# Buffers of their own for some streamed weights, and work laid into other places, in a hybrid SSD and attention decoder block

## The chip, the cores and the metric

The kernel runs on one core of a Trainium2 chip. The metric is the device time of one execution in microseconds (us). A core has five engines that this text names: PE (TensorE, the matrix products), DVE (VectorE), ACT (ScalarE), POOL (GpSimd) and SP (SyncE, which here does nothing but issue DMA transfers). Each engine works through its own instructions in order and waits at a semaphore where it needs another's result. "Issued in order" holds for SP as well: a transfer that must wait for its buffer holds up all that stand behind it in SP's queue.

## The reference, cut to what matters

One decoder block, sequence 1024, width 1024, everything in float32:

```
h     = rms_norm(x) * (1 + sc1) + sh1                  # sc, sh, g from the condition c
z, xbc, dt, q, k, v, gates = split(h @ w_in)
y_ssd = ssd_branch(z, xbc, dt)                         # causal conv, softplus(dt), chunked scan, silu(z), norm
y_att = diff_attention_branch(q, k, v)                 # rope, causal softmax, difference of two heads, norm
merged = sig(gate_ssd) * (y_ssd @ w_ssd_o) + sig(gate_att) * (y_att @ w_attn_o)
x  = x + g1 * rms_norm(merged @ w_out)
h2 = rms_norm(x) * (1 + sc2) + sh2
u  = causal_dwconv(h2 @ w_up)                          # 3 taps, 2 * 2816 channels
x  = x + g2 * rms_norm((gelu(u_gate) * u_val) @ w_down)
```

Inside the SSD branch, `dt = softplus(dt_raw + dt_bias)`, `la = -dt * exp(a_log)` and its running sum `acum` over chunks of 128 give the decays.

## The kernel before, in words

**Products.** A float32 product is made of three products in the rounded type fp32r: `split(hi, lo, raw)` (lines 93 and 94) lets ACT copy `raw` to a rounded `hi` and DVE subtract to get `lo`; `mm3` (lines 115 to 117) issues hi·hi, hi·lo and lo·hi into the same PSUM bank. Weights come by SP's DMA queue as a raw piece of 128 partitions x 1024, and are split. Most pieces rotate through pools: three buffers with the tag `wraw`, four each for `whi` and `wlo`. A load into a `wraw` buffer waits until the split has read what was there.

**Slots.** Longer-lived tensors take one of 43 slots (128 x 1024 float32) from `SL`: `get` takes the front of a list of free slots, `put` appends to its end. A tensor that takes a slot waits for whoever used it last, and which slot it is depends on all gets and puts before it.

**Order.** Inside `manual_schedule(engines=...)` the instructions of the named engines stay in the order in which the code is written; elsewhere a scheduler lays them out. Of the stages below, z is manual on PE, DVE, ACT and SP. The stages in order of time in the trace: h and first products (0 to 75 us), xbc and others (75 to 214), z (214 to 331), the SSD scan and v (from 331), gates, q and k, attention, attention's output product (about 1100 to 1185), the product with `w_out` ("mix"), norm and h2, the up-projection (about 1290 to 1712), the down-projection (to the end).

**z** (lines 529 to 578) runs over three thirds of the columns (346, 346, 348); each third needs four pieces of weights (`kp` 0 to 3, each two blocks of 128 rows), and runs over eight token tiles `i` of 24 matmuls. `fetch_z` loads a piece (line 531), `split_z` splits it. Three pieces of the next third are fetched at tile 1, and split after tile 7; the fourth is fetched after the first split, which frees its buffer. After each tile ACT takes a tanh (line 574), DVE a product (575), in the first third also the dt columns (570), and SP stores the result (576). In the second third three functions are called after tiles 1, 3 and 5: `decays_a` (23 elementwise operations, lines 484 to 503), `decays_b` (two matmuls that sum `la` along the chunk, 505 to 517), `decays_c` (eight transposes, 519 to 525). POOL sums parts of w_down (lines 415 to 418) beside all this.

**Start of the scan.** After z the slots of `ev`, `wdr` and `wds` go back to the list, and `yt`, `xd`, `xdd`, `xtk`, `M`, ... take slots.

**Attention's output product** "ao" (lines 1300 to 1321) runs over eight blocks `j` of two halves with 24 matmuls each. `fetch_ao` (1189) loads the weights `wao` two blocks ahead, `split_ao` splits them. `gth` (1303) and `mst` (1304) are loaded per block; DVE merges (1319, 1320) into `mt`, which is split into `mT[j][half]`, the operand of mix. Beside it, in blocks 0 to 2 `early_load` brings two pieces of w_up (`ws`, 1283) and `early_sums` makes four sums of them on DVE (1288 to 1291), stored to memory; in blocks 3 to 6 a piece of `w_out` (`wo`, 1313) is loaded and split. All of these use the three `wraw` buffers.

**Up-projection**: 22 pairs `m` of blocks, each made in seven products `p` (a Strassen-like scheme) of 12 matmuls into banks X, Z, X, Y, X, Y, X; ACT and DVE combine the banks (lines 1826 to 1849: `cv`, `evs`, `cg`). A pair's conv steps (`up_conv` 0 to 4: steps 0 and 2 start with an ACT pass, line 1436, all of 0 to 3 have a DVE tap, 1437, then gelu, 1439; step 4 multiplies, 1441, and stores, 1446 and 1447) and its four sums (`up_gsum`, 1455, stored 1457) are laid into places (m, p) of later pairs. For the early pairs that is the list `early` (lines 1804 to 1811). The last pair's are in the list `rest` (1868), inside the first of the down products.

**Down-projection**: seven products over six pieces `kp`; 24 matmuls per full piece. `left_part` (line 1756) loads a piece of the gelu product or its sums back through two `gst` buffers and splits it; `right_part` loads from w_down (`wdb`) or from POOL's sums (`wdt`, 1767).

Of the kernel before, what the change touches and what calls it, by code (L numbers as in the profile page):

```python
# [17 lines left out]
P = 128  # L18
# [43 lines left out]
def kernel(ctx: ExitStack, tc: tile.TileContext, a: dict, out: bass.AP, dbg=None):  # L62
# [422 lines left out]
    def decays_a():  # L485
        t0 = f(sp0_)
        t1 = sp1_
        x_ = f(dtr)
        V.scalar_tensor_tensor(t0, x_, -1.0, x_, op0=ALU.mult, op1=ALU.min)
        A.activation(t0, t0, AF.Exp)  # L490
        V.tensor_scalar(t1, t0, 2.0, None, op0=ALU.add)
        V.reciprocal(t1, t1)
        V.tensor_tensor(t0, t0, t1, op=ALU.mult)
        V.tensor_tensor(t1, t0, t0, op=ALU.mult)
        dtf = f(dt)
        V.tensor_scalar(dtf, t1, 2.0 / 15, 2.0 / 13, op0=ALU.mult, op1=ALU.add)
        for m in (11, 9, 7, 5, 3, 1):
            V.tensor_tensor(dtf, dtf, t1, op=ALU.mult)
            V.tensor_scalar(dtf, dtf, 2.0 / m, None, op0=ALU.add)
        V.tensor_tensor(dtf, dtf, t0, op=ALU.mult)  # L500
        V.scalar_tensor_tensor(dtf, x_, 0.0, dtf, op0=ALU.max, op1=ALU.add)
        A.activation(aexp, rows[:, R_AL : R_AL + NH], AF.Exp)
        V.scalar_tensor_tensor(la, dt, -1.0, aexp[:, None, :].broadcast_to([P, 8, NH]), op0=ALU.mult, op1=ALU.mult)

# [21 lines left out]

    thirds = ((0, 346), (346, 346), (692, 348))
# [12 lines left out]
    z_raw = [fetch_z(*thirds[0], kp) for kp in range(3)]  # L540
    with tc.manual_schedule(engines={EN.PE, EN.DVE, EN.Activation, EN.SP}):
        for t_, (c0, wdt) in enumerate(thirds):
            if t_ == 0:
                wz = []
                for kp in range(4):
                    wz.append(split_z(c0, wdt, kp, z_raw.pop(0)))
                    if kp == 0:
                        z_raw.append(fetch_z(c0, wdt, 3))
            else:
                wz = wz_next  # L550
            for i in range(8):
# [7 lines left out]
                if t_ < 2 and i == 1:  # L559
                    z_raw = [fetch_z(*thirds[t_ + 1], kp) for kp in range(3)]  # L560
                if t_ < 2 and i == 7:
                    wz_next = []
                    for kp in range(4):
                        wz_next.append(split_z(*thirds[t_ + 1], kp, z_raw.pop(0)))
                        if kp == 0:
                            z_raw.append(fetch_z(*thirds[t_ + 1], 3))
# [634 lines left out]
    with tc.manual_schedule(engines={EN.PE, EN.DVE, EN.Activation, EN.Pool}):  # L1201
# [71 lines left out]
        mT = [[new_hl(f"mT{k}_{h}") for h in range(2)] for k in range(KD)]  # L1273
# [728 lines left out]
```

## Time and profile before

| | |
|---|---|
| median of 3 runs | 1930.75 us (1929.4 to 1933.46) |
| profiled execution | 1933.49 us, span in the trace 1931.7 us |
| TensorE's mean granted clock | 0.99 |
| PE busy | 1869.5 us, 97% of the span |
| DVE, ACT, POOL busy | 1209.6, 850.4, 215.4 us |
| DMA | 309.48 MB, mean 160 GB/s |

Times in the profile are microseconds from the start of the span. "L531" is line 531 of the program; "out<-in" names the tensors. "idle before <-releaser" tells how long an engine had waited and whose work ended the wait. PE stands for the matmuls, PEld for the weight loads that run beside them; PEclk is the clock that the throttle granted to TensorE, 1.00 being full speed. SPq is the time in which SP issues a transfer; a DMA row in the chain of waits is the time from issue to landing.

### The profile page before, as it was taken

What the parts mean: (1) busy time and instruction counts of PE and PEld (TensorE: products, weight loads), DVE (VectorE), ACT (ScalarE), POOL (GpSimd) and SP (SyncE); (2) the same over time, 40 slices, a digit from 0 to 9 for tenths busy, and PEclk for the clock granted to TensorE, in tenths of its full rate; (3) what the DMA queues carried; (4) which work ended last, traced back from release to release, by engine and by line L of the source; (5) the groups of instructions that cost most, each with busy time, mean ns of one, the idle gap of its engine ahead of it and who ended that gap; (6) DMA issues with size and microseconds to landing.
All of it is one profiled execution on the core that took longest, in us unless ns stands there. A gap on an engine that the chain in (4) does not pass through costs nothing.

```text
span 1931.7 us, 24508 instructions
## 1 busy us (share of the span) xinstructions
PE 1869.5 (97%) x9128; PEld 1560.1 (81%) x9128; DVE 1209.6 (63%) x1815; ACT 850.4 (44%) x1628; POOL 215.4 (11%) x225
## 2 busy tenths in 40 slices
PE   6999979999999999999999999999999999999998
PEld 4787978788888888888888778887788888878886
DVE  6957343575326326667767546368998888886545
ACT  5522122655313215565556413266555455455532
POOL 0000252454261000000000010100000000000001
PEclk8999989999999999999999999999999999999999
DMA  9834365142666745665572368122332232368754
GB/s 304 275 112 144 120 207 174 51 136 80 248 234 147 242 168 152 176 178 154 158 191 81 111 229 284 69 84 77 115 109 103 104 115 92 108 228 290 244 156 158
DMA packets 135575, 309.48 MB, mean 160 GB/s; under 512 B 17056, under 2 KB 48416, under 8 KB 135456
## 3 DMA queue, kind: packets, MB, share of 16 engines
q1 hardware_dynamic: 127808, 281.65, 45.5%
q0 software_dynamic: 7648, 26.26, 3.9%
q8 instruction: 72, 1.18, 0.2%
q14 instruction: 47, 0.39, 0.1%
HBM read 218.97 MB, written 88.88 MB: 159 GB/s over the span
## 4 chain that ended last, share of the span: by engine, by line
PE 80%; DVE 8%; ACT 5%; DMA 4%; issue 2%; SPq 1%; POOL 0%; POOLq 0%; ACTq 0%; DVEq 0%
PE upx L1420 4%; PE upx L1421 4%; PE upx L1419 3%; PE o L1125 3%; PE xbc L115 2%; PE xbc L116 2%; PE xbc L117 2%; PE upy L1420 2%; PE upy L1419 2%; PE upy L1421 2%; PE dx L1783 2%; PE dx L1784 2%; PE dx L1782 2%; PE dy L1784 2%; PE dy L1782 2%
## 5 line engine op out<-in xcount | busy, mean ns | idle before, releaser
L1419 PE MATMUL upx<-t,wu_t 128*128 128x512 f32 x264 | 103.2, 391 | 1.5 <-DVE cv L1845 1.5
L1420 PE MATMUL upx<-t,wu_t 128*128 128x512 f32 x264 | 102.8, 390 | 0.2 <-DVE t L1537 0.2
L1421 PE MATMUL upx<-t,wu_t 128*128 128x512 f32 x264 | 102.8, 389 | 0.0
L1113 ACT COPY aT<-at 128x512 f32<-128x512 f32 (+2 forms) x96 | 46.1, 481 | 103.1 <-PE at L1112 103.1
L1393 ACT ACTIVATE wu_t<-sab 128x512 fp32r<-128x512 f32 x57 | 34.1, 628 | 124.6 <-DVE sab L1410 124.6
L1125 PEld LDWEIGHTS o<-vt,aT 128*128 128x128 f32 x576 | 74.6, 191 | 10.1 <-ACT aT L1113 6.1
L1125 PE MATMUL o<-vt,aT 128*128 128x128 f32 x576 | 80.9, 277 | 0.5 <-ACT aT L1113 0.3
L94 DVE TENSOR_TENSOR g_lo<-gst,g_hi 128x1024 fp32r<-128x1024 f32 (+1 forms) x42 | 47.6, 1134 | 45.0 <-ACT g_hi L93 44.9
L142 POOL TENSOR_TENSOR rsf<-rsf,nhalf 128x1 f32<-128x1 f32 x8 | 5.6, 705 | 627.3 <-DVE rsf L141 624.6
L115 PE MATMUL z<-wz_hi,hT 128*128 128x346 f32 (+1 forms) x192 | 65.2, 339 | 7.5 <-ACT wz_hi L93 7.5
L93 ACT ACTIVATE g_hi<-gst 128x1024 fp32r<-128x1024 f32 (+1 forms) x42 | 41.6, 990 | 64.9 <-DMA gst<-gld_s 28.3
L142 POOL TENSOR_TENSOR sqt<-sqt,nhalf 128x4 f32<-128x4 f32 x16 | 16.6, 1035 | 465.6 <-DVE sqt L141 465.6
L1086 DVE TENSOR_REDUCE nmx<-sc 128x1 f32<-128x640 f32 (+3 forms) x64 | 65.6, 1025 | 2.2
L116 PE MATMUL z<-wz_lo,hT 128*128 128x346 f32 (+1 forms) x192 | 64.7, 337 | 1.7 <-DVE wz_lo L94 1.7
L117 PE MATMUL z<-wz_hi,hT 128*128 128x346 f32 (+1 forms) x192 | 64.1, 334 | 0.0
L1066 PE MATMUL sc<-kst,qst 128*128 128x512 f32 (+2 forms) x192 | 63.8, 340 | 0.0
L115 PE MATMUL xbc<-hT,wx_hi 128*128 128x512 f32 x160 | 63.5, 397 | 0.0
L1067 PE MATMUL sc<-klo,qst 128*128 128x512 f32 (+2 forms) x192 | 63.2, 346 | 0.0
L117 PE MATMUL xbc<-hT,wx_lo 128*128 128x512 f32 x160 | 62.3, 389 | 0.0
L116 PE MATMUL xbc<-hT,wx_hi 128*128 128x512 f32 x160 | 62.2, 389 | 0.0
L1437 DVE SCALAR_TENSOR_TENSOR ug<-cg,vec,ug 128x1023 f32<-128x1023 f32 (+1 forms) x44 | 56.3, 1281 | 6.1 <-ACT ug L1436 5.0
L1419 PEld LDWEIGHTS upx<-t,wu_t 128*128 128x128 f32 x264 | 49.6, 188 | 12.9 <-DVE cv L1845 2.6
(449 smaller groups left out, 5859.0 us busy)
## 6 DMA issues: line engine op xcount, KB each, us to landing
adas<-in_w_ada SPq DMA_DIRECT2D x32, 512.0 KB, 5.0
wdr<-in_w_down POOLq DMA_DIRECT2D x22, 512.0 KB, 7.0
wtd<-wds POOLq DMA_DIRECT2D x22, 512.0 KB, 4.6
wuf<-in_w_up SPq DMA_DIRECT2D x22, 512.0 KB, 3.5
gld_s<-gsum SPq DMA_DIRECT2D x22, 512.0 KB, 2.8
gst<-gld_s SPq DMA_DIRECT2D x20, 512.0 KB, 4.4
wdt_raw<-wtd SPq DMA_DIRECT2D x20, 512.0 KB, 4.7
wuv<-in_w_up SPq DMA_DIRECT2D x19, 512.0 KB, 3.6
```

The source lines that it names most:

```text
L115: T.matmul(ps, lh, rh, start=(i == 0), stop=False)
L116: T.matmul(ps, lh, rl, start=False, stop=False)
L117: T.matmul(ps, ll, rh, start=False, stop=(i == n - 1))
L1066: T.matmul(sc[:, n0:n1], qs_[s][:, tsl], ks_[s][:, n0:n1], start=True, stop=False)
L1067: T.matmul(sc[:, n0:n1], qs_[s][:, tsl], kl[s][:, n0:n1], start=False, stop=True)
L1086: V.reduce_max(nmx[:, bq, s : s + 1], sc[:, :L], axis=AX.X, negate=True)
L1125: T.matmul(po_of[j, grp][:, qi, :], at[:, k, :], vt[j % 2][:, kt, :], start=(kt == 0), stop=(kt == i))
L1419: T.matmul(out_, wh, xh_, start=(k == 0 and first), stop=False, skip_group_check=not first)
L1420: T.matmul(out_, wh, xl_, start=False, stop=False, skip_group_check=not first)
L1421: T.matmul(out_, wl, xh_, start=False, stop=(k == end), skip_group_check=not first)
L1782: T.matmul(o, gh[:, kk, tsl], wh, start=(k == 0 and not more), stop=False, skip_group_check=more)
L1784: T.matmul(o, gl[:, kk, tsl], wh, start=False, stop=(k == KF - 1), skip_group_check=more)
```

## The change

It has five parts, called A to E in what follows.

A. z's fourth piece gets a slot of its own, `zraw`, taken before the block and put back after it, and is fetched together with the other three.

```diff
     def fetch_z(c0, wdt, kp):
-        raw = wp.tile([P, 2, wdt], F32, tag="wraw", name=f"wz{c0}_{kp}_raw", bufs=3)
+        raw = zraw[:, :, :wdt] if kp == 3 else wp.tile([P, 2, wdt], F32, tag="wraw", name=f"wz{c0}_{kp}_raw", bufs=3)
...
-    z_raw = [fetch_z(*thirds[0], kp) for kp in range(3)]
+    zraw = SL.get("zraw", F32, (P, 2, HALF))
+    z_raw = [fetch_z(*thirds[0], kp) for kp in range(4)]
...
                 if t_ < 2 and i == 1:
-                    z_raw = [fetch_z(*thirds[t_ + 1], kp) for kp in range(3)]
+                    z_raw = [fetch_z(*thirds[t_ + 1], kp) for kp in range(4)]
                 if t_ < 2 and i == 7:
                     wz_next = []
                     for kp in range(4):
                         wz_next.append(split_z(*thirds[t_ + 1], kp, z_raw.pop(0)))
-                        if kp == 0:
-                            z_raw.append(fetch_z(*thirds[t_ + 1], 3))
...
-    SL.put(*ev, *wdr, *wds)
+    SL.put(*ev, *wdr, *wds, zraw)
```

B. `decays_a` becomes a generator with a `yield` after each of its operations; six of them are issued after each of the tiles 0 to 4 of the second third. `decays_b` follows tile 6, `decays_c` tile 1 of the last third.

```diff
-                if t_ == 1 and i in (1, 3, 5):
-                    (decays_a, decays_b, decays_c)[i // 2]()
+                if t_ == 1 and i < 5:
+                    dec = dec or decays_a()
+                    for _ in range(6):
+                        next(dec, None)
+                elif t_ == 1 and i == 6:
+                    assert next(dec, None) is None
+                    decays_b()
+                elif t_ == 2 and i == 1:
+                    decays_c()
```

SP's queue in the first third of z: the stores `zd` of its tiles and the four loads for the second third (the last third's stand alike). Before:

```order
L576 DMA zd_622<-ev_1614 128x330
L531 DMA wz_0_raw<-in_w_zdt 128x2x346
L531 DMA wz_1_raw<-in_w_zdt 128x2x346
L531 DMA wz_2_raw<-in_w_zdt 128x2x346
L576 DMA zd_623<-ev_1615 128x330
L576 DMA zd_624<-ev_1614 128x330
L576 DMA zd_625<-ev_1615 128x330
L576 DMA zd_626<-ev_1614 128x330
L576 DMA zd_627<-ev_1615 128x330
L576 DMA zd_628<-ev_1614 128x330
L531 DMA wz_3_raw<-in_w_zdt 128x2x346
L576 DMA zd_629<-ev_1615 128x330
```

After:

```order
L587 DMA zd_622<-ev_1614 128x330
L545 DMA wz_0_raw<-in_w_zdt 128x2x346
L545 DMA wz_1_raw<-in_w_zdt 128x2x346
L545 DMA wz_2_raw<-in_w_zdt 128x2x346
L545 DMA zraw<-in_w_zdt 128x2x346
L587 DMA zd_623<-ev_1615 128x330
L587 DMA zd_624<-ev_1614 128x330
```

The fourth load moved up by six stores, to stand with the other three.

C. In ao, the `ws` loads and the second half's `wo` pieces get slots of their own, a pair of `ws` is summed one block after its load, `wo` is loaded two pieces ahead, and `mT`'s slots are taken block by block.

```diff
-        mT = [[new_hl(f"mT{k}_{h}") for h in range(2)] for k in range(KD)]
+        mT = [[None] * 2 for _ in range(KD)]
...
-            ra, rb = [wp.tile([P, 2, HALF], F32, tag="wraw", name=f"ws{m}_{i}", bufs=3) for i in range(2)]
+            ra, rb = [SL.get(f"ws{m}_{i}", F32, (P, 2, HALF)) for i in range(2)]
...
+        def wo_load(kp):
+            if kp < 4:
+                wo_raw.append(SL.get(f"wo1_{kp}_raw", F32, (P, 2, HALF)))
+                SP.dma_start(wo_raw[-1], a["w_out"][2 * kp * P : (2 * kp + 2) * P, HALF:].rearrange("(k p) c -> p k c", p=P))
...
             if j < 3:
-                early_sums(j, *early_load(j))
-            elif j < 7:
-                kp = j - 3
-                raw = wp.tile([P, 2, HALF], F32, tag="wraw", name=f"wo1_{kp}_raw", bufs=3)
-                SP.dma_start(raw, a["w_out"][2 * kp * P : (2 * kp + 2) * P, HALF:].rearrange("(k p) c -> p k c", p=P))
+                ws_raw.append(early_load(j))
+            if 0 < j < 4:
+                early_sums(j - 1, *ws_raw.popleft())
+            if j == 3:
+                wo_load(0)
+                wo_load(1)
+            elif j > 3:
+                kp = j - 4
                 wo[1][kp] = (new_hl(f"wo1_{kp}_hi"), new_hl(f"wo1_{kp}_lo"))
+                raw = wo_raw.popleft()
                 split(*wo[1][kp], raw)
+                SL.put(raw)
+                wo_load(kp + 2)
```

SP's queue around the start of ao. `stg` loads attention's outputs back, `gad` holds the gates. Before:

```order
L1171 DMA stg_8245<-atd_676 128x512
L1028 DMA gad_660<-gev 128x512
L1304 DMA mst<-msd_662 128x1024
L1028 DMA gad_661<-gev 128x512
L1303 DMA gth_8784<-gad_654 128x1024
L1283 DMA ws_0_8822<-in_w_up 128x1024
L1028 DMA gad_661<-gev 128x512
L1283 DMA ws_1_8823<-in_w_up 128x1024
L1189 DMA wao_raw<-in_w_attn_o 128x1024
L1283 DMA ws_0_8899<-in_w_up 128x1024
L1303 DMA gth_8784<-gad_655 128x1024
L1304 DMA mst<-msd_663 128x1024
```

After:

```order
L1189 DMA stg_8243<-atd_676 128x512
L1046 DMA gad_660<-gev 128x512
L1301 DMA ws_0_8954<-in_w_up 128x1024
L1324 DMA wo_0_raw<-in_w_out 128x2x512
L1324 DMA wo_2_raw<-in_w_out 128x2x512
L1301 DMA ws_0_8875<-in_w_up 128x1024
L1046 DMA gad_661<-gev 128x512
L1301 DMA ws_1_8955<-in_w_up 128x1024
L1207 DMA wao_raw<-in_w_attn_o 128x1024
L1324 DMA wo_1_raw<-in_w_out 128x2x512
L1046 DMA gad_661<-gev 128x512
L1324 DMA wo_3_raw<-in_w_out 128x2x512
```

All six `ws` and the four `wo` loads now stand ahead of the second block's `gth` load; before, three of the six `ws` stood ahead of it, the others among the loads of blocks 1 and 2, and the `wo` at blocks 3 to 6.

D. The list for early pairs has 26 entries instead of 25.

```diff
-        early = [[x_] for x_ in early] + [[(up_conv, 1, 4), (up_gsum, 1, 0)], [(up_gsum, 1, i) for i in range(1, 4)]]
-        early += [[(up_conv, 2, i)] for i in range(5)] + [[(up_conv, 3, i)] for i in range(4)]
-        early += [[(up_conv, 3, 4), (up_gsum, 3, 0)], [(up_gsum, 3, 1), (up_gsum, 3, 2)], [(up_conv, 4, 0), (up_gsum, 3, 3)]]
-        early += [[(up_conv, 4, i)] for i in range(1, 5)]
+        early = [[x_] for x_ in early] + [[(up_conv, 1, 4)], [(up_gsum, 1, 0), (up_gsum, 1, 1)], [(up_gsum, 1, 2), (up_gsum, 1, 3)]]
+        early += [[(up_conv, 2, i)] for i in range(5)] + [[(up_conv, 3, i)] for i in range(5)]
+        early += [[(up_gsum, 3, 0), (up_gsum, 3, 1)], [(up_gsum, 3, 2), (up_conv, 4, 0)], [(up_conv, 4, 1), (up_gsum, 3, 3)]]
+        early += [[(up_conv, 4, i)] for i in range(2, 4)] + [[(up_conv, 4, 4), (up_conv, 5, 0)]]
```

From pair 3 on a step comes one or two products later. In pair 5, for instance, the first steps of conv 4 stood at products 2 and 3 and stand at 3 and 4. ACT's order there, `ug` being the pass of the conv step, the rows on line 1842 (1875) the copy of bank Y. Before:

```order
L1826 COPY cv_10261<-upx_10687 128x512
L1828 COPY evs_10039<-upx_10823 128x512
L1393 ACTIVATE wu_t_10860<-sab_10443 128x512
L1393 ACTIVATE wu_b_10881<-sab_10443 128x512
L1436 ACTIVATE ug_10444<-cg_10260,vec 128x1024
L1839 COPY evs_10039<-upx_10823 128x512
L1393 ACTIVATE wu_t_10902<-wuv_10726 128x512
L1842 COPY evs_10039<-upy_10888 128x512
```

After:

```order
L1859 COPY cv_10259<-upx_10684 128x512
L1861 COPY evs_10037<-upx_10820 128x512
L1426 ACTIVATE wu_t_10854<-sab_10441 128x512
L1426 ACTIVATE wu_b_10875<-sab_10441 128x512
L1872 COPY evs_10037<-upx_10820 128x512
L1426 ACTIVATE wu_t_10895<-wuv_10721 128x512
L1469 ACTIVATE ug_10442<-cg_10258,vec 128x1024
L1875 COPY evs_10037<-upy_10881 128x512
```

The pass `ug` moved from ahead of the copy of X to right ahead of the copy of Y.

E. The last pair's steps are spread over six pieces of the first down product instead of four.

```diff
-        rest = [[(up_conv, m, 0), (up_conv, m, 1)], [(up_conv, m, 2), (up_conv, m, 3)], [(up_conv, m, 4), (up_gsum, m, 0), (up_gsum, m, 1)], [(up_gsum, m, 2), (up_gsum, m, 3)]]
+        rest = [[(up_conv, m, i)] for i in range(4)] + [[(up_conv, m, 4), (up_gsum, m, 0)], [(up_gsum, m, i) for i in range(1, 4)]]
```

More of the change, by code (lines that the diff above doesn't have):

```diff
@@ L546 @@
                     wz.append(split_z(c0, wdt, kp, z_raw.pop(0)))
-                    if kp == 0:
-                        z_raw.append(fetch_z(c0, wdt, 3))
             else:
@@ L564 @@
                         wz_next.append(split_z(*thirds[t_ + 1], kp, z_raw.pop(0)))
-                        if kp == 0:
-                            z_raw.append(fetch_z(*thirds[t_ + 1], 3))
                 lo = 0
@@ L1294, in early_sums @@
                 G.dma_start(wsd[m][i][:, 1], y_)
+            SL.put(ra, rb)
         gth = SL.get("gth2")
@@ L1299 @@
         fetch_ao(1)
+        ws_raw, wo_raw = deque(), deque()
+        def wo_load(kp):
+            if kp < 4:
+                wo_raw.append(SL.get(f"wo1_{kp}_raw", F32, (P, 2, HALF)))
+                SP.dma_start(wo_raw[-1], a["w_out"][2 * kp * P : (2 * kp + 2) * P, HALF:].rearrange("(k p) c -> p k c", p=P))
         for j in range(KD):
@@ L1320 @@
                 V.tensor_tensor(mt[:, hsl], mt[:, hsl], mst[:, hsl], op=ALU.add)
+                mT[j][half] = new_hl(f"mT{j}_{half}")
                 split(mT[j][half][:, 0, :], mT[j][half][:, 1, :], mt[:, hsl])
@@ L1878 @@
                         left_part(1, kp)
-                    for f_, *x_ in rest[kp] if kp < len(rest) else ():
+                    for f_, *x_ in rest[kp]:
                         f_(*x_)
```

16 lines of the change are left out of this document (15 added, 1 removed).

## The prediction

> **What bounds the kernel now.** I read the busy shares first, then the waits of TensorE (PE), then the chain of waits and timelines at the places the change touches. The page:
>
> ```profile
> span 1931.7 us, 24508 instructions
> PE 1869.5 (97%) x9128; PEld 1560.1 (81%) x9128; DVE 1209.6 (63%) x1815; ACT 850.4 (44%) x1628; POOL 215.4 (11%) x225
> PE 80%; DVE 8%; ACT 5%; DMA 4%; issue 2%; SPq 1%; POOL 0%; POOLq 0%; ACTq 0%; DVEq 0%
> ```
>
> PE is the bound: 97% busy. The change leaves every matmul in, so time can only come out of PE's idle stretches and out of matmuls that ran slowly behind them. PE's waits (us in total, times, longest):
>
> ```profile
> PE z L115 <- ACT wz_hi L93: 7.5, 2, 4.7
> PE acum_ps L507 <- DVE sm L503: 5.3, 1, 5.3
> PE ao L115 <- ACT wao_hi L93: 4.5, 2, 4.2
> PE pb L711 <- ACT M L715: 1.7, 1, 1.7
> PE upx L1419 <- DVE cv L1845: 1.5, 2, 1.3
> PE dx L1783 <- DVE wdb_lo L94: 1.3, 1, 1.3
> ```
>
> The first three belong to the stages that parts A, B and C edit. What a wait costs on top is seen in the stretches around them (us, then PE, PEld, DVE, ACT, POOL busy, PE's granted clock, DMA share, GB/s):
>
> ```profile
> 251.20:258.00 6.80, 4.57 (x14) 4.20 (x15) 2.37 (x4) 1.69 (x3) 6.16 (x8) 0.50 0.15 56
> 271.60:278.50 6.90, 4.92 (x18) 4.92 (x19) 3.75 (x11) 0.79 (x3) 2.91 (x5) 0.51 0.73 232
> 299.00:305.80 6.80, 6.06 (x21) 6.06 (x22) 1.63 (x3) 0.46 (x1) 2.88 (x3) 0.50 0.71 250
> 1144.00:1152.50 8.50, 3.83 (x10) 2.63 (x10) 3.90 (x5) 2.19 (x3) 0.54 (x1) 0.80 0.86 293
> ```
>
> After each long wait the clock is half for about 6.8 us, which loses up to 3.4 us of full speed; in the fourth row 0.80 over 8.5 us is one half-clock stretch of 3.4 us, a loss of 1.7. That is why the waits alone (some 15 us in z) understate z.
>
> **Part A and B, z.** The chain of waits (start, us, what):
>
> ```profile
> 243.25 0.89 DVE wz_lo L94
> 244.16 7.71 DMA wz_raw<-in_w_zdt
> 251.95 0.79 ACT wz_hi L93
> 252.76 1.28 DVE wz_lo L94
> ...
> 267.12 1.21 DVE sm L499
> ...
> 273.24 0.30 DVE sm L503
> 273.58 0.79 PE acum_ps L507 x2
> ...
> 291.55 5.78 DMA wz_raw<-in_w_zdt
> ...
> 298.23 1.47 DVE wz_lo L94
> ```
>
> The fourth transfer of a third is issued at 244.16, only when the split of the first piece has ended and freed a buffer; it takes 7.71 us, and PE meets the split at 251.95. At 291.55 the same again. At 273.24 PE waits for decays_a's last piece, since acum's matmuls stand in PE's order two tiles behind a chain of 23 operations, two of them on ACT, the rest on DVE. What all of it costs is read from ACT's tanh rows, which mark the tiles:
>
> ```profile
> 237.95 0.45 ACT L574 ACTIVATE ev<-z 128x330 f32<-128x330 f32 x1 [3.35 <-DVE sm L570]
> 241.75 0.45 ACT L574 ACTIVATE ev<-z 128x330 f32<-128x330 f32 x1 [3.35 <-DVE sm L570]
> 326.30 0.46 ACT L574 ACTIVATE ev<-z 128x348 f32<-128x348 f32 x1 [3.32 <-PE z L117]
> ```
>
> An undisturbed tile takes 241.75 − 237.95 = 3.80 us. From tile 6 of the first third (241.75) to tile 6 of the last (326.30) are 16 tiles: 84.55 us instead of 60.8, so 23.75 lost. About 1.6 of it are the matmuls of acum and acT at full clock (rows 0.79 and 0.43, the first at half clock, and as many again for acT), which stay. Left to win: 22 (the first third's fourth piece is asked for before the block and costs PE nothing today).
>
> Does it go? With its own slot the fourth piece is issued at tile 1, six tiles or some 23 us before its split; 7.71 us fit. The split must still wait for the last product of tile 7 to free the split buffer (four of them); then ACT 0.79 and DVE 0.89 to 1.47 follow, and PE needs it after six of the next tile's eight row blocks, 3.80 × 6/8 = 2.85 us later. So 0.6 to 1.2 us are spare: no stall, but a thin margin. The decays: six operations per tile of 3.80 us, mostly 0.3 us, at worst 1.21 (row 267.12), so 1.8 to 7.3 us in a tile where DVE otherwise works some 0.7. At the worst price they run past a tile, but the two PSUM buffers and two tiles up to decays_b (tile 6) absorb it. Behind those pieces wait the tanh products and the release of PSUM; a tile's own DVE work comes first in the order. I take A and B at −22, bounds −23.75 (all loss goes) and −14 (one wait of 4.7 with its 3.4 of clock stays, 8.1 less).
>
> A's price: one slot more is taken and put back, so later tensors get another slot.
>
> ```profile
> 330.86 0.59 ACT L696 COPY xtk<-px 128x512 f32<-128x512 f32 x1
> ...
> 336.82 1.14 ACT L715 ACTIVATE M<-pb,sm 128x128 f32<-128x128 f32 x4 [2.76 <-DMA zd<-ev]
> ```
>
> M takes today the slot of the last z tile and waits for its store to land, while the xtk copy at 330.86 went ahead. One slot on, it is xtk that waits for the store: its 0.59 and a copy of 0.27 behind it come after the landing, +0.9 (0 to +2.7, the wait shown, if more falls behind it). It ends in PE's pb wait of 1.7.
>
> By the Trainium skill, GPSIMD Engine Reference, "1. Specifications", GpSimd shares its SBUF interface with VectorE and contends with instructions that have two SBUF inputs; that speaks against A, whose last lo split has two. The trace agrees: 0.89 at 243.25, and 1.28 at 252.76, in the stretch from 251 with POOL busy 6.16 of 6.80 us. By the rule alone, with POOL's work on that split, the margin is the 0.6 and not the 1.2; a kept wait would make it 1914, which is the second rival below.
>
> **Part C, the output product.** VectorE's rows at block 0 and block 5, and the chain's transfer:
>
> ```profile
> 1111.54 0.69 DVE L1319 SCALAR_TENSOR_TENSOR mt<-gth,ao 128x512 f32<-128x512 f32 x1 [1.67 <-PE ao L117]
> 1175.26 0.69 DVE L1319 SCALAR_TENSOR_TENSOR mt<-gth,ao 128x512 f32<-128x512 f32 x1 [0.83 <-PE ao L117]
> ...
> 1133.16 6.48 DMA ws<-in_w_up
> ```
>
> A 512-column matmul has a pitch of 0.2267 (twelve in 2.72 us, from 1402.19 to 1404.91 below). Five blocks of 48 are 54.4 us; 63.72 passed, 9.3 lost, of which seven mix matmuls laid between take 1.6. The ws loads wait for wraw buffers and land 6.48 us later, VectorE stands in front of its sum, and everything behind it on DVE, SP and ACT (mt, gth, the wao load, the wao split) is late: PE waits 4.5 and then runs at 0.80. Now the ws and wo loads have slots and go out in SP's order ahead of this stage, and a sum comes one block after its load. All of the wao path then keeps its usual lead. −7.2 (0.5 of small waits kept), bounds −9.3 and 0.
>
> What SP is moved past: ten loads of 512 KB now stand earlier among stg, gad and wao loads. At the 293 GB/s of the row at 1144 they are 5.2 MB, 18 us of transfer; they cost nothing as long as the loads behind them are due later than that. mT's slots are now taken block by block, which frees slots and delays nothing.
>
> **Part D, early pairs.** No work is added; conv steps and sums move one to three products later, so pair 3's cv copy no longer stands behind three sums (wait 1.3 goes, 0.2 stays). Pair 5:
>
> ```profile
> 1397.41 1.25 ACT L1436 ACTIVATE ug<-cg,vec 128x1024 f32<-128x1024 f32 x1 [1.44 <-DVE gsum L1455]
> 1398.57 0.56 ACT L1839 COPY evs<-upx 128x512 f32<-128x512 f32 x1
> 1399.71 0.59 ACT L1842 COPY evs<-upy 128x512 f32<-128x512 f32 x1
> ...
> 1402.19 0.39 PE L1419 MATMUL upy<-b,wu_b 128*128 128x512 f32 x1
> 1404.91 0.42 PE L1419 MATMUL upx<-t,wu_t 128*128 128x512 f32 x1
> ```
>
> Today ug's ACT pass goes ahead of both copies of banks, and the Y copy ends at 1400.30, 1.9 before PE needs Y at 1402.19. Now ug stands directly before the Y copy and itself waits for a sum (two DVE sums of 0.7, then 1.25 and 0.59): done about 1402.8, PE waits 0.6. The cv copy of the next product and pair 6 lose about 1 each, pairs 3 and 4 some 0.4 each. Sum +3.6 − 1.3 = +2.3; bounds −1.3 (none is late) and +4 (each copy late by one ACT pass, 1.25 × 4, less 1.3).
>
> **Part E, the last pair.** Two kp steps later (2 × 24 × 0.2267 = 10.9 us) a12's last column is stored.
>
> ```profile
> 1725.37 4.57 DMA gst<-gld_a
> 1731.06 1.23 DVE g_lo L94
> ...
> 1761.31 0.43 SPq L1767 DMA_DIRECT2D wdt_raw<-wtd  x1
> ...
> 1769.50 1.06 ACT L93 ACTIVATE wdt_hi<-wdt_raw 128x1024 fp32r<-128x1024 f32 x1 [3.35 <-DMA wdt_raw<-wtd]
> 1774.05 0.39 PE L1782 MATMUL dx<-wdt_hi,g_hi 128*128 128x512 f32 x1
> ```
>
> The wait of 1.3 in the first product (behind the product and sums of the pair) goes. But the left operands run through two gst buffers, a round of 4.57 + 1.06 + 1.23 = 6.9, 3.4 for each piece. SP's queue now holds one such piece more ahead of the first wdt load (1761.31 today). wdt_hi is ready at 1770.56, 3.5 before 1774.05, lo about 2.2 before. One piece and the 0.5 of issue: 3.9 later than today, so PE waits 1.7 for lo; with the later g_hi behind it 3.3. Net +2 with the 1.3 taken off; bounds −1.3 (no new wait) and +3.4 (two pieces: 6.9 − 2.2 = 4.7, less 1.3).
>
> **Sum.** −22 − 7.2 + 0.9 + 2.3 + 2 = −24.0. The profiled execution took 1933.49 (span 1931.7 and 1.8 around it), 2.7 above the median of 1930.75; its own time becomes 1909.5, the median 1906.8: 1907.
>
> **Rivals.**
> - Nothing is given back: the slots move nobody, copies and wdt arrive in time. −22 − 7.2 − 1.3 − 1.3 = −31.8: 1899. For it: the new waits are small against spare times of 1.9 and 2.2; against it: three queues (ACT, DVE, SP) each would have to hide it.
> - One of the large waits stays: the lo split of the fourth piece misses its 0.6 us, or the wao loads stay late in a stretch at 0.86 of DMA capacity. One wait of 4.2 to 4.7 with its slow clock, 6 to 8: 1914. Against it: 23 us of lead.
> - A new wait lets the clock fall too. The smallest wait here that was followed by half clock is z's second, 7.5 − 4.7 = 2.8 us (stretch from 299); a wdt wait of 3.3 would do it and cost 3.4 more: 1912. By the Trainium skill, TensorE: Matmul & The Clock Gate, "What's actually happening", an idle window of about 3.4 us, free-running, throttles, and as long a busy one releases; by that a wait of 2 us alone would not. The rows (0.50 after 4.7 and 2.8) neither need nor refuse the windows being fixed in time.
> - Slower: the ten moved loads stand in SP's queue waiting for slots that attention still uses, and wao, gth and stg loads behind them come late, with PE waiting. C's 7.2 is then not won, and A, B, D, E leave −16.8; it decides when the block keeps PE over 16.8 us. All 18 us of transfer with 3.4 of half clock behind them give +4.6: 1935. For it: the order has all ten ahead of the second block's gth load. Against it: DMA moved 56 to 293 GB/s in the stretches shown, so there is room, and a transfer of 6 to 8 us has a lead of tens.
> - The change moves nothing: the scheduler gives the loads their old places, and another buffer than wraw binds the fourth split: 1931. The order shows the loads moved, so only z could stand still.
>
> **How the numbers follow.** The forecast case has 0.70 (1902 to 1910 by itself, from D's and E's bounds); nothing given back 0.09; one wait stays 0.08; the clock falls as well 0.08; no change 0.03; slower 0.02. 0.2% is 3.9 us, about what a measurement of this kernel can tell from no change; all but the last two cases lie over it: faster 0.95, same 0.03, slower 0.02. The range reaches from the case without givebacks, 1899, to 1917: one kept wait at its dearest (8.1) and 2 of D's upper bound above the forecast.
>
> **What would show it.** Right: no PE wait on wz_hi or acum_ps in z, tiles of 3.80 us throughout and a clock of 1.00 from 225 to 310; ao without the wait on wao_hi; small waits on evs or cv in pairs 3 to 6 and on wdt_hi or wdt_lo at the third down product. Wrong: waits of over 2 us in z or ao again, a wait of ao on gth or wao with SP held at a ws load, or a new wait of over 4 us in the tail.

## The result, and the profile after

The changed kernel took 1905.93 us (median of four runs, 1905.24 to 1907.22), the kernel before 1930.52 on the same chip (four runs, 1929.4 to 1933.46). The ratio is 0.9871 with a 95% interval of 0.9854 to 0.9888, so 24.6 us or 1.3% faster. The forecast was 1907.

The page of the changed kernel, with the clock that the throttle granted in 40 slices (every slice at 9 now; before, two of the first seven stood at 8):

```profile
span 1903.5 us, 24513 instructions
PE 1860.1 (98%) x9128; PEld 1552.4 (82%) x9128; DVE 1205.6 (63%) x1815; ACT 848.8 (45%) x1628; POOL 213.0 (11%) x225
PEclk9999999999999999999999999999999999999999
```

PE's waits after (us in total, times, longest), those in the stages that the change touches:

```profile
PE px L711 <- DVE sm L716: 1.9, 1, 1.9
PE upy L1452 <- ACT evs L1875: 1.3, 2, 1.1
PE upx L1452 <- DVE cv L1878: 1.0, 2, 0.8
PE upx L1452 <- ACT evs L1872: 0.6, 1, 0.6
PE dx L1816 <- DVE wdb_lo L94: 0.4, 1, 0.4
```

The three large ones (wz_hi 7.5, acum_ps 5.3, wao_hi 4.5) are gone. Four of the five small ones stand where the prediction put a loss; the wait for wdb_lo, which it said would go, is left with 0.4. Two of z's stretches that ran at half clock, now (columns as before: us; PE, PEld, DVE, ACT, POOL busy; PE's clock; DMA share; GB/s):

```profile
251.20:258.00 6.80, 6.80 (x45) 6.80 (x44) 5.97 (x10) 1.47 (x4) 5.79 (x7) 1.00 0.90 269
299.00:305.80 6.80, 6.80 (x45) 6.80 (x45) 1.14 (x3) 1.70 (x4) 0.10 (x1) 1.00 0.45 180
```

PE is busy for all of both at full clock, with 45 matmuls where 14 and 21 stood.

By stages (from the first matmul of one stage to the first of the next, z to the start of its last, in the two profiled executions; worked out from the starts of PE's rows):

| stage | before | after | difference |
|---|---|---|---|
| up to z | 214.29 | 214.82 | +0.5 |
| z, first to last matmul | 115.44 | 92.69 | −22.7 |
| start of the scan, to its first product | 12.37 | 12.79 | +0.4 |
| scan to the end of attention | 758.36 | 758.15 | −0.2 |
| ao and mix | 151.90 | 144.16 | −7.7 |
| norm and h2 | 34.26 | 34.26 | 0.0 |
| up-projection | 425.73 | 428.40 | +2.7 |
| down-projection to the end | 219.38 | 218.18 | −1.2 |
| span | 1931.7 | 1903.5 | −28.2 |

The spans differ by 28.2, the medians by 24.6. The profiled execution of before was the slowest of its four (1933.46 as timed, 2.9 above their median), that of after the fastest (0.7 below): 3.6 of the difference lie in which executions were profiled. In which stage before lost its 2.9 is not known, as only one of its executions has a trace.

### The profile page after: what moved, and what is told of

Read it like the earlier page. It is cut to its first block, busy times and chain, and to the rows that moved or that the text cites. A ratio compares the mean times of both kernels' runs of the same rounds, so it can differ in the third digit from the quotient of the medians.

```text
span 1903.5 us, 24513 instructions
## 1 busy us (share of the span) xinstructions
PE 1860.1 (98%) x9128; PEld 1552.4 (82%) x9128; DVE 1205.6 (63%) x1815; ACT 848.8 (45%) x1628; POOL 213.0 (11%) x225
## 4 chain that ended last, share of the span: by engine, by line
PE 77%; DVE 9%; DMA 5%; ACT 5%; POOL 2%; issue 2%; SPq 1%; POOLq 0%; ACTq 0%; DVEq 0%
PE upx L1453 3%; PE upx L1452 3%; PE upx L1454 3%; PE o L1143 3%; PE xbc L115 2%; PE xbc L116 2%; PE xbc L117 2%; DMA wdr<-in_w_down 2%; PE dx L1816 2%; PE dx L1817 2%; PE dx L1815 2%; PE dy L1816 2%; PE dy L1817 2%; PE dy L1815 2%; PE v L667 2%
## 5 line engine op out<-in xcount | busy, mean ns | idle before, releaser
L115 PE MATMUL z<-wz_hi,hT 128*128 128x346 f32 (+1 forms) x192 | 62.1, 323 | 0.0
L117 PE MATMUL z<-wz_hi,hT 128*128 128x346 f32 (+1 forms) x192 | 61.4, 320 | 0.0
```

The lines of the kernel that those rows point to most:

```text
L115: T.matmul(ps, lh, rh, start=(i == 0), stop=False)
L117: T.matmul(ps, ll, rh, start=False, stop=(i == n - 1))
```

## The experiments

The experiments ran in three groups, each beside the kernel before on one chip; the medians of before there were 1932.14 (e1 to e4), 1932.63 (e5 to e8) and 1930.74 (e9 to e11), so a time is best read against those.

**e1, part A alone.**

```diff
+        raw = zraw[:, :, :wdt] if kp == 3 else wp.tile([P, 2, wdt], F32, tag="wraw", name=f"wz{c0}_{kp}_raw", bufs=3)
...
+    zraw = SL.get("zraw", F32, (P, 2, HALF))
...
+                    z_raw = [fetch_z(*thirds[t_ + 1], kp) for kp in range(4)]
...
+    SL.put(*ev, *wdr, *wds, zraw)
```

> The kernel before with part A alone (own slot for z's fourth piece; decays, ao, early and last pairs as before). Theory, the losses are separate events and add up: in the trace of before the two late fourth pieces lost 8.1 us (225 to 262) and 7.2 us (285 to 331) beyond the pitch of PE's matmuls, clock included; A takes both out and nothing else, and the start of the scan loses 0.4 to 0.9 by the shifted slot: 1930.5 - 15.3 + 0.6 = 1916, with PE's wait of 5.3 for the decays still there. Rival, the decays were late because VectorE was held up by the late split: the wait of 5.3 goes as well and A alone gives nearly all of z's 22, 1909. Rival, the slow clock was not tied to these waits: only the waits themselves go, 4.7 + 0.7 + 2.8 + 1.1 = 9.2, 1921.

1916.39 (1913.91 to 1919.1), ratio 0.9918 (0.9904 to 0.9931), 15.8 under before. The sum came out as the theory had it, but by other terms. z shrank by 18.8 us in the trace, not 15.3, and the start of the scan lost 2.1, not 0.6. PE's waits of this kernel:

```profile
PE px L690 <- DVE sm L695: 2.3, 1, 2.3
PE acum_ps L507 <- DVE sm L503: 1.7, 1, 1.7
PE z L116 <- DVE wz_lo L94: 1.4, 2, 0.7
```

The wait for the decays fell from 5.3 to 1.7 though the decays were not touched. So the waits were not separate. GpSimd's last sum at the decays' start and its next one, and one of VectorE's rows of the decays, of this kernel:

```profile
255.70 1.30 POOL L418 TENSOR_TENSOR wds<-wdr,wds 128x512 f32<-128x512 f32 x1
263.64 1.29 POOL L415 TENSOR_TENSOR wds<-wdr 128x512 f32<-128x512 f32 x1 [4.53 <-DMA wdr<-in_w_down]
```

```profile
260.44 0.23 DVE L499 TENSOR_SCALAR sm<-sm 128x128 f32<-128x128 f32 x1
```

Here most of the decays ran in GpSimd's pause between 257 and 263.6. Before, with PE late by a wait, GpSimd's sums from 266.88 to 272.4 lay on the decays' last steps, and rows of 0.23 to 0.30 took 1.2 to 1.3. Experiment e8 tests that. The scan's start lost more than a slot's shift: behind the wait of 2.3 the clock fell, in the second of these stretches of this kernel (us, PE, PEld, DVE, ACT, POOL, clock, DMA share, GB/s):

```profile
316.88:320.29 3.41, 1.07 (x10) 0.79 (x8) 1.13 (x2) 1.89 (x7) 1.04 (x1) 1.00 0.78 289
320.29:323.70 3.41, 3.41 (x13) 2.85 (x11) 2.85 (x5) 3.38 (x9) 1.65 (x2) 0.50 0.02 5
```

3.41 us at 0.50 lose up to 1.7, and the wait is 0.6 longer (2.3 against 1.7): that covers the 2.1.

**e2, part B alone** (the loads of z as before, the `yield`s in `decays_a` as changed).

```diff
-                if t_ == 1 and i in (1, 3, 5):
-                    (decays_a, decays_b, decays_c)[i // 2]()
+                if t_ == 1 and i < 5:
+                    dec = dec or decays_a()
+                    for _ in range(6):
+                        next(dec, None)
...
```

> The kernel before with part B alone (decays in pieces; the fourth piece still through the three shared buffers). Theory of separate events: the excess of 7.9 us between 262 and 285 less the 0.8 of matmuls that stay goes, 1930.5 - 7.1 = 1923, with both waits for wz_hi still there. Rival, the decays hide under the late split anyway or VectorE's pieces delay that split further: within 1 us of before, 1930. Rival of the clock: the wait of 5.3 goes without its clock loss, 1925.

1924.96 (1923.56 to 1927.54), ratio 0.9959 (0.9946 to 0.9973), 7.2 under before, the size of the theory's 7.1. The stall at acum is gone, and the first late fourth piece stands; at the second change of third, though, the wait for wz_hi that the theory kept is gone too, and others stand in its place:

```profile
PE z L115 <- ACT wz_hi L93: 4.4, 1, 4.4
PE z L116 <- DVE wz_lo L94: 3.1, 4, 1.5
PE z L115 <- DVE ev L589: 2.0, 1, 2.0
```

The wait of 2.0 is for a tile's PSUM: VectorE's product waited to reuse `ev`, whose store took long, as this kernel's chain of waits shows:

```profile
290.61 10.35 DMA zd<-ev
300.98 0.02 DVEq L589
301.05 0.53 DVE ev L589
```

**e3, part C alone.**

```diff
-            ra, rb = [wp.tile([P, 2, HALF], F32, tag="wraw", name=f"ws{m}_{i}", bufs=3) for i in range(2)]
+            ra, rb = [SL.get(f"ws{m}_{i}", F32, (P, 2, HALF)) for i in range(2)]
...
+            if 0 < j < 4:
+                early_sums(j - 1, *ws_raw.popleft())
...
```

> The kernel before with part C alone (slots of their own beside the output product, sums one block later). Theory: ao's excess of 7.6 us beyond the pitch goes, 1930.5 - 7.6 = 1923, no PE wait on wao_hi. Rival, the loads beside it collide with the transfers of attention's end or need the slots as A shifts them: half of it or less, 1927 or above, with a wait somewhere ahead of ao.

1922.95 (1922.01 to 1925.21), ratio 0.9953 (0.9941 to 0.9965), 9.2 under before, 6.8 to 11.4 by the interval. In the trace the stage from ao to the norm lost 7.7 us, as in after, and no wait on wao_hi is left; z's waits stand as before:

```profile
PE z L115 <- ACT wz_hi L93: 8.5, 2, 4.9
PE acum_ps L507 <- DVE sm L503: 4.2, 1, 4.2
```

C owes nothing to the slots that A shifts. A, B and C alone give 15.8, 7.2 and 9.2, in sum 32.1; together, with E but without D (e4), 29.4. They don't quite add up, and need not: 3.6 of the decays' wait is taken away by A as well as by B.

**e4, part D undone** in the changed kernel (the list `early` as in the kernel before).

```diff
-        assert len(early) == 26
+        assert len(early) == 25
...
+        early += [[(up_conv, 4, i)] for i in range(1, 5)]
```

> The changed kernel with the list of early pairs as it was before. Theory: the waits on evs and cv in pairs 3 to 6 (1.1, 0.8, 0.6 and some 0.8 in small ones) come from the moved steps and go, the wait of pair 3 for cv (1.3) and 0.2 come back: 2.7 us less in the up-projection, 1905.9 - 2.7 = 1903.2. Rival, the waits come from slots that A and C shifted, not from D's places: they stay, 1906 or 1907. Rival, the part was needed since the pair-3 wait grows when the loads behind C come earlier: slower than 1906.

1902.77 (1902.17 to 1904.22), 3.2 under after's 1905.93; the up-projection takes 425.75 in the trace, 2.65 less. The waits of D are gone and the old one is back; further on, two stand that after does not have so:

```profile
PE upx L1452 <- DVE cv L1878: 1.5, 2, 1.3
...
PE dx L1816 <- DVE wdt_lo L94: 0.8, 1, 0.8
PE dx L1816 <- DVE wdb_lo L94: 0.8, 1, 0.8
```

The theory holds as to the place: the loss comes from D's moved steps. The size is not the waits alone, which fell by 1.3 (from 1.06, 0.82, 0.59 and two below 0.15 to one of 1.30). By the starts of PE's rows, each wait also lengthens the two distances between matmuls at its end by some 0.27 together: the 1.06 at 1372.82 cost 1.33. Counted so, as excess over the pitch, D's places take 4.1 in after and 1.6 in e4.

**e5, part E undone** in the changed kernel.

```diff
-        rest = [[(up_conv, m, i)] for i in range(4)] + [[(up_conv, m, 4), (up_gsum, m, 0)], [(up_gsum, m, i) for i in range(1, 4)]]
+        rest = [[(up_conv, m, 0), (up_conv, m, 1)], [(up_conv, m, 2), (up_conv, m, 3)], [(up_conv, m, 4), (up_gsum, m, 0), (up_gsum, m, 1)], [(up_gsum, m, 2), (up_gsum, m, 3)]]
...
+                    for f_, *x_ in rest[kp] if kp < len(rest) else ():
```

> The changed kernel with the last pair's steps in four pieces as before (part E undone). Theory, E costs nothing: in the trace of after the first wdt load goes out 20.4 us after the second product's start instead of 17.2, 3.2 later, but wdt_hi is ready 1.5 us before PE wants it, while the first product's wait falls from 1.3 to 0.4. Undoing E then gives 0.9 us back: 1906.8. Rival, the prediction's step (a net price of 2): undoing it gains, 1904. Rival, it is a matter of when transfers land (in the run without D a wait of 0.8 for wdt_lo and one of 0.8 for wdb_lo stood there): no difference beyond 0.5, 1906.

1905.8 (1904.74 to 1906.23): no difference, the second rival; the theory's 0.9 does not show in the time. PE's wait in the first down product is 1.0 here, 0.4 with E.

**e6, D undone and ev's slots put back last.**

```diff
-    SL.put(*ev, *wdr, *wds, zraw)
+    SL.put(*wdr, *wds, zraw, *ev)
```

> The changed kernel without D, and with ev's two slots put back last after z (SL.put(*wdr, *wds, zraw, *ev)). Theory, the wait of px at the start of the scan (1.9 in after, 1.5 without D) is xtk waiting for the last z store in a slot that ev left; with a slot of wdr or wds, whose stores landed long before, it goes: 1902.8 - 1.6 = 1901. Rival, xtk is also held by ACT's wv splits, so that less than 0.5 comes: 1902.5. Rival, the other slots make a later tensor wait for the same store (M or prev): no gain, 1903.

1901.08 (1899.34 to 1902.32), ratio 0.9836 (0.9815 to 0.9857). The wait on px is gone, and from the last z matmul to the scan's first product PE needs 10.36 us in the trace, against 12.79 after and 12.37 before. So also the kernel before lost 2 us there, under another name (pb <- M).

**e7, the same without E** (the edits of e6 and of e5 together).

> The same kernel as the one before it in this call, with part E undone as well. Theory, E costs nothing here either: within 1 us of that kernel, above it by 0.9 if the wait of 1.3 in the first down product comes back. Rival, E's late wdt loads cost as much as the prediction said: 2 us below it.

1902.04 (1901.29 to 1902.2), 1.0 above e6, which ran beside it; the two ranges overlap. Its trace has the wait of the first down product back at 1.3, where e6 has 0.3:

```profile
PE dx L1816 <- DVE wdb_lo L94: 1.3, 1, 1.3
```

With e5, E is worth between 0 and 1 us; it does not cost 2.

**e8, GpSimd's sums left out in z**, in the kernel before.

```diff
-        G.tensor_tensor(t1, b12, b11, op=ALU.subtract)
...
+        if not no_sums:
+            G.tensor_tensor(t1, b12, b11, op=ALU.subtract)
...
+    for t in wds:
+        G.memset(t, 0.0)
```

> The kernel before, with GpSimd's four sums of w_down left out in the six calls inside z (its transfers stay; zeros are stored instead). Theory, GpSimd's sums slowed VectorE in the decays: with them away the row L499 stays at 0.23 (1.20 to 1.31 in before), the 23 steps end 3.6 us earlier as they do with A alone, where the sums fell elsewhere, and PE's wait on sm L503 falls from 5.3 to 1.7 with its half clock gone: 1930.5 - 3.6 - 2.4 = 1924.5. Rival, the steps of the chain hang on each other and on their operands' size: the wait stays at 5 and the time at 1930. Rival, the transfers were the reason (they stay here): also no change.

1921.26 (1914.78 to 1922.29), ratio 0.9935 (0.9911 to 0.996), 11.4 under before, where 6 were expected. A step of the decays (line 502 here) and PE's waits:

```profile
264.99 0.23 DVE L502 TENSOR_SCALAR sm<-sm 128x128 f32<-128x128 f32 x1
```

```profile
PE z L115 <- ACT wz_hi L93: 2.0, 1, 2.0
...
PE acum_ps L510 <- DVE sm L506: 1.3, 1, 1.3
```

All six rows of that line that the decays issue are at 0.23, and the wait fell from 5.3 to 1.3. GpSimd's loads were all issued by 248.81 here, ahead of the decays (DMA share 0.00 from 262 to 266), so this run alone does not part its sums from its transfers. The kernel before does. In the first of these stretches of it the DMA engines are fully busy, and the decays' rows that start there take 0.23 to 0.29; in the second DMA is nearly idle, GpSimd sums, and four rows take 1.2 to 1.3 (columns as in e1):

```profile
263.50:266.80 3.30, 3.30 (x23) 3.30 (x22) 2.96 (x11) 0.46 (x1) 0.00 (x0) 1.00 1.02 375
266.80:272.40 5.60, 1.50 (x10) 1.22 (x8) 5.43 (x6) 0.46 (x1) 5.11 (x5) 0.93 0.18 65
```

So GpSimd's sums slowed VectorE. Each of the four slowed rows starts within a sum and ends 0.08 to 0.15 us behind that sum's end, as this one, again of the kernel before:

```profile
268.65 1.26 POOL L416 TENSOR_TENSOR wds<-wdr,wds 128x512 f32<-128x512 f32 x1 [0.41 <-DMA wdr<-in_w_down]
268.68 1.31 DVE L499 TENSOR_SCALAR sm<-sm 128x128 f32<-128x128 f32 x1
```

That the wait for the fourth piece fell too, from 7.5 to 2.0, was not foreseen: its transfers took 5.06 and 3.13 us in this run instead of 7.71 and 5.78. Together z is 15.6 us shorter in the trace, while ao and the start of the scan are 2.4 and 1.0 longer. GpSimd's own loads went out at other times here; which of their meetings made the fourth piece quicker stays open.

**e9, the slot without the lead**: the fourth piece in `zraw`, but loaded at tile 7.

```diff
-                    z_raw = [fetch_z(*thirds[t_ + 1], kp) for kp in range(4)]
+                    z_raw = [fetch_z(*thirds[t_ + 1], kp) for kp in range(3)]
                 if t_ < 2 and i == 7:
+                    z_raw.append(fetch_z(*thirds[t_ + 1], 3))
```

> The changed kernel, with z's fourth piece still in its own slot but loaded only at tile 7, ahead of the splits, instead of at tile 1. Theory, what counts is the lead of the load, and the slot only allows it: SP issues it about 1 us after tile 7's start, it lands 5.8 to 7.7 later (the two transfers of before), the split takes 0.8, and PE wants it 6.65 after the tile's start: waits of 1 to 3 us at each change of third, with half clock behind the longer one, 3 to 9 us slower than after, 1909 to 1915. Rival, the buffer was all: 1906.

1912.61 (1911.7 to 1913.13), 6.7 over after; z took 98.95 us in the trace instead of 92.69. The chain of waits at the second change of third, and PE's wait:

```profile
274.45 7.40 DMA zraw<-in_w_zdt
...
281.94 0.79 ACT wz_hi L93
```

```profile
PE z L115 <- ACT wz_hi L93: 2.7, 1, 2.7
```

At the first change the same load took 3.68 and PE waited only 0.4 for lo. So the buffer was not all: the lead of six tiles, which the slot allows, is worth 6.3 of z's time. It is not all either: with part B alone (e2) z takes 107.33, 8.4 more than here, where the load has a slot but no lead. Without a buffer to wait for it goes out at 243.16 instead of 244.59, and it took 3.68 instead of 7.42; how much of the 8.4 is the luck of these transfers is open. The wait of 2.7 was followed by matmuls at half clock (0.29 apart instead of 0.158).

**e10, the ws sums in the block of their load**, the loads in slots as changed.

```diff
-            if 0 < j < 4:
-                early_sums(j - 1, *ws_raw.popleft())
+                early_sums(j, *ws_raw.popleft())
```

> The changed kernel, with the sums of ws in the block of their load again (early_sums(j) at j), the loads in slots of their own as changed. Theory, the slots are what takes VectorE's stall out, since the scheduler then sends the loads ahead of ao and they have landed long before: same as after, 1906. Rival, the block between load and sum is needed too: VectorE waits for a ws load in blocks 0 to 2 and PE for wao_hi, 2 to 8 us slower.

1906.01 (1904.27 to 1907.21), the same as after, and ao and mix take 144.16 us again. The block between load and sum did none of C's work. What stays in this kernel, the slots of ws and wo, wo's loads ahead and mT's later slots, was not tried apart; the prediction's reason speaks for the slots.

**e11, e6 with one of pair 1's three sums moved a place on.**

```diff
-        ... [(up_gsum, 1, i) for i in range(1, 4)]]
-        early += [[(up_conv, 2, i)] for i in range(5)] ...
+        ... [(up_gsum, 1, 1), (up_gsum, 1, 2)]]
+        early += [[(up_gsum, 1, 3), (up_conv, 2, 0)]] + [[(up_conv, 2, i)] for i in range(1, 5)] ...
```

> The kernel of e6 (without D, ev put last) with pair 1's sums moved in a smaller way: one of the three sums at place (3, 4) goes to (3, 5), together with the first step of conv 2; nothing after it moves. Theory, PE's wait of 1.3 on cv at pair 3 stands behind three sums of 0.6 on VectorE, so one sum less takes 0.6 out: 1901.1 - 0.6 = 1900.5, within what can be measured of e6; in the trace cv's wait at pair 3 falls to 0.7. Rival, conv 2's step then delays cg one product later: cv's wait is traded for one on cg, no gain or a loss of up to 1.3.

1899.81 (1899.28 to 1901.18), ratio 0.9838 (0.9825 to 0.9852) to before, 30.9 us. The wait fell as reckoned:

```profile
PE upx L1452 <- DVE cv L1878: 0.9, 2, 0.7
```

The up-projection is only 0.05 us shorter than in e6 (425.70 against 425.75), though: nearly all of what cv no longer waits is given back in small pieces. Against e6 the 1.3 us between the medians cannot be told from nothing, but this kernel is 6.1 us faster than the changed one and the fastest of all here.

## Why the prediction was right, point by point

**PE's waits carry the gain.** Right: the 97% went to 98%. z and the output product with mix gain 30.4 us in the traces, more than the whole 28.2; the other stages together take 2.2 back.

**A and B, −22.** The size was right (−22.2 to the end of z, −22.7 for z itself), and tiles run at 1.00 of clock. Two of its steps were loose, and the cause that it gave for the decays' wait was mostly another. It summed the stage as a whole, which is why it survived what e1 and e8 found: the wait for the decays was not simply a chain two tiles too long. Of its 5.3 us, 1.3 to 1.7 are the chain (e8, e1), and the rest came from GpSimd's sums, which lay on it in the kernel before. In the changed kernel two of the pieces still take 1.33 and 1.26 beside the sums (at 253.15 and 254.51), and PE does not wait. The row at 267.12 stood in the prediction as a price for the pieces, and was not read as the cause. The margin of the last split came out: at the two changes lo was ready 1.1 and 0.7 us before its first matmul, where 0.6 to 1.2 were reckoned. VectorE's row of the changed kernel at the first (that matmul starts at 248.62):

```profile
246.63 0.88 DVE L94 TENSOR_TENSOR wz_lo<-zraw,wz_hi 128x692 fp32r<-128x692 f32 x1
```

By the Trainium skill's GPSIMD Engine Reference, "1. Specifications", GpSimd's SBUF interfaces are shared with VectorE, with contention for VectorE's instructions in a 2-port perf mode or with two SBUF inputs. The two-input split that the prediction weighed does meet the sums with part A alone (e1): at the second change of third it took 1.96 and a sum beside it 1.93, and PE waited 0.7 twice:

```profile
281.10 1.93 POOL L418 TENSOR_TENSOR wds<-wdr,wds 128x512 f32<-128x512 f32 x1
281.80 1.96 DVE L94 TENSOR_TENSOR wz_lo<-zraw,wz_hi 128x696 fp32r<-128x696 f32 x1
```

In the changed kernel GpSimd pauses there (273.00 to 278.66) and the split takes 0.88; no part of the change places GpSimd's sums, so the margin held by luck of timing, which repeats (z takes 92.7 us in all seven traces with A and B and the early load). What cost most before was another case: L499, with one SBUF operand, went from 0.23 to 1.31 beside the sums and back to 0.23 in e8. Whether L499 runs in such a mode, no run here shows.

**The scan's start, +0.9.** It cost 0.4 in the stage, in the way described: xtk waits for the last z store.

```profile
309.25 5.04 DMA zd<-ev
314.29 0.02 issue
314.31 0.04 ACTq L714
```

In e1 the same shift cost 2.1, up to 1.7 of it half clock; in e6 a different order of puts took 2.4 away. The bounds of 0 to 2.7 were needed.

**C, −7.2.** −7.7 by the trace, and alone −7.7 as well (e3). The reason given, loads that waited for shared buffers, fits e3 and e10, though the slots were not tried apart from wo's lead and mT's later slots; that a sum one block later mattered was wrong (e10).

**D, +2.3.** +2.7 by the trace, 3.2 by the times. The mechanism stood as worked out, though its terms add up to 3.4 and not 3.6 (0.6, two of 1, two of 0.4), and 5 − 1.3 to an upper bound of 3.7. Pair 5, ACT, then PE:

```profile
1371.05 1.24 ACT L1469 ACTIVATE ug<-cg,vec 128x1024 f32<-128x1024 f32 x1 [3.58 <-DVE gsum L1488]
1372.20 0.56 ACT L1875 COPY evs<-upy 128x512 f32<-128x512 f32 x1
```

```profile
1372.82 0.50 PE L1452 MATMUL upy<-b,wu_b 128*128 128x512 f32 x1 [1.06 <-ACT evs L1875]
1376.66 0.50 PE L1452 MATMUL upx<-t,wu_t 128*128 128x512 f32 x1 [0.82 <-DVE cv L1878]
```

ug waits for a sum, the copy of Y stands behind ug, and PE waits 1.06 where 0.6 was reckoned, then 0.82 for cv where about 1 was. The terms left out the 0.27 that each wait costs on top (e4), and the smaller waits came out below them.

**E, +2: the step that failed.** It measured −1.2 (0 to −1.0 in e5 and e7). Part of that is scatter: over all 13 traces the down-projection takes 217.6 to 219.6 with E and 218.8 to 219.9 without. The later wdt load was right: it goes out 20.4 us after the second product's start instead of 17.2, so 3.2 later where 3.9 was reckoned. SP's, ACT's and PE's rows:

```profile
1736.30 0.43 SPq L1800 DMA_DIRECT2D wdt_raw<-wtd  x1
1743.25 1.06 ACT L93 ACTIVATE wdt_hi<-wdt_raw 128x1024 fp32r<-128x1024 f32 x1 [2.55 <-DMA wdt_raw<-wtd]
1745.83 0.39 PE L1815 MATMUL dx<-wdt_hi,g_hi 128*128 128x512 f32 x1
```

It landed 6.9 us after issue, less than the 8.2 before, so hi was ready 1.5 us early and lo just in time. The further 1.6 for a late g_hi had no row behind it and did not come. So the prediction's wait of 1.7 for lo failed on two sizes: it took the load's 8.2 us as fixed, and it had lo lose 3.9 of its 2.2 to spare, where it lost about 2. In e4 and e9 the wait for wdt_lo was there, with 0.8. The margin is about half a microsecond.

**The sum** of −24.0 met the medians' −24.6 partly by luck. The profiled execution of before was 2.7 above the median, and against its own trace the terms were 4.2 too small: 3.2 of it E, 0.7 z, 0.5 C and 0.5 the scan's start, less 0.4 in D and 0.3 in the stages without a term.

**The clock.** No wait above 1.9 us is left from z on, and no slice is below 9 tenths. The prediction took 2.8 us as the smallest wait that half clock follows; that was too high. (By its own terms that rival comes to 1906.8 + 3.4 = 1910, not 1912.) Half clock followed a wait of 2.3 in e1 (above), of 2.0 in e2 and of 1.9 in e8, but not the 1.9 of the changed kernel nor 2.3 in e10.

The traces show what decides. The granted clock changes only at points of a grid: in the kernel before it fell at 251.17, 271.65, 298.96 and 1148.87, which lie 6, 8 and 249 times 3.413 us apart, and it stayed at half for one or two such steps. Every trace has that grid, at an offset of its own. Half clock followed where a wait emptied enough of one step. In the 13 traces, from 45 us after the start to 12 us before the end, there are 16 steps at full clock in which PE idled 1.91 us or more, and half clock followed each; it followed none in which PE idled 1.73 or less. The wait of 1.9 in e8 (for pb, ended at 324.46) lies within one step, and that of the changed kernel (ended at 315.52) is cut by a grid point into 1.04 and 0.89. e8's two steps, then those of the changed kernel:

```profile
322.53:325.94 3.41, 1.50 (x12) 1.40 (x12) 1.53 (x3) 3.35 (x10) 0.32 (x1) 1.00 0.23 87
325.94:329.36 3.42, 3.42 (x14) 3.04 (x13) 2.29 (x3) 3.36 (x11) 1.80 (x2) 0.50 0.20 77
```

```profile
311.25:314.66 3.41, 2.37 (x11) 1.61 (x9) 1.29 (x2) 0.85 (x3) 0.00 (x0) 1.00 0.91 337
314.66:318.07 3.41, 2.52 (x14) 1.91 (x15) 2.60 (x3) 3.35 (x12) 2.08 (x2) 1.00 0.37 139
```

The prediction left open whether the windows are fixed in time; here they are. By the Trainium skill, TensorE: Matmul & The Clock Gate, "What's actually happening", the window is 3413 ns and free-running; the grid of these traces agrees. But the page has half clock come after at least one idle window, and here 1.91 us within a window were enough, with matmuls before and behind. The measurement decides.

## What to carry to other kernels

When a load waits for a shared buffer, look for the lead it loses: 6.7 us of the slot's worth came only with the load issued six tiles earlier (e9), and moving a consumer later added nothing once the load had its lead (e10). Sum a stage as a whole, clock and all, before dividing it among its waits, because one wait sets how the other engines' work falls on each other. And for each part of a change that moves steps without removing work, follow the two or three instructions queued directly behind the moved one: that priced part D to within half a microsecond or so, and undoing D (e4) showed that it was better left out.

## What the runs showed that was not expected

- Whether a PE wait of some 2 us is followed by 3.41 us of half clock, which adds up to 1.7 us, hangs on where it falls: 1.91 us within one step of a 3.413 us grid were followed by it (e8), 2.25 cut into 0.62 and 1.63 were not (e10). Between 1.73 and 1.91 these traces have no case.
- GpSimd's elementwise sums (128 x 512) made VectorE's 128 x 128 steps with one SBUF operand take up to 1.31 us instead of 0.23; in the decays of the kernel before a slowed step ended just behind the sum it started in. With the sums taken out all were at 0.23 again (e8).
- The order in which slots are returned was worth about 2 us where the next stage takes them at once: 12.79 us against 10.36 for the same work (after, e6).
- The load of z's fourth piece (128 x 692 or 696) took between 3.1 and 7.7 us from issue to landing (e8, before), so a load at tile 7 is sometimes early enough and sometimes not: in e9 PE waited 0.4 us for the split at one change of third and 2.7 at the other. The quick one went out at 243.16, ahead of GpSimd's next transfers, the slow one at 274.45, behind four that GpSimd issued from 271.13 on; no run tests that.
